# Both feed-forward networks of a decoder layer: gate and up as Strassen's seven products, down as a stage of its own

## The chip, the cores and the metric

One core of one Trainium2 chip runs the whole layer as one program. The metric is the device time of one execution in microseconds (us). TensorE (PE) multiplies matrices into PSUM; VectorE (DVE), ScalarE (ACT) and GpSimd (POOL) do elementwise work; SyncE (SP) issues the DMAs, all on one queue.

## The reference

One step of a decoder layer over 1,024 prompt tokens and 64 sample tokens, 1,088 in all, with a model width of 1,024. The change touches the two half-step feed-forward networks (FFNs), before the token mixing and after it:

```python
def swiglu_half(x, norm_g, w_gate, w_up, w_down):
    u = rmsnorm(x, norm_g)
    return x + 0.5 * ((jax.nn.silu(u @ w_gate) * (u @ w_up)) @ w_down)

h = swiglu_half(x, *ffn1)
# ... input projection, two kinds of windowed attention, cross attention ...
h = swiglu_half(h, *ffn2)
y = rmsnorm(h, final_norm)
```

w_gate and w_up are 1,024 x 2,816, w_down is 2,816 x 1,024. All data are float32.

## The kernel before, in words

Activations lie transposed: model width on the 128 partitions (8 blocks k), tokens along the free axis, in three chunks CH of 384, 384 and 320 tokens. Each float32 operand is split in two parts of TensorE's rounded format, high = round(a) on ScalarE and low = a - high on VectorE, and each product is three matmuls (`mm3`: high x high, high x low, low x high). Weights pass through the class `Weights`: a list `entries` in the order of use, each 128 x 1024; `load` puts the DMA on SP's queue into one of two raw buffers, `split` makes the parts in one of four ring buffers (lines 75 and 76), and `done` frees a ring buffer and goes on with the next.

`ffn` works on one block m of 128 hidden units at a time, 22 in all. The gate of a block: 3 chunks x 8 k x 3 matmuls with the weight block stationary and up to 384 tokens moving, into PSUM. The evacuation (lines 303 to 305) multiplies by the tokens' 1/rms (`rbc`), applies silu and multiplies by `rbc` again; the gain is already in the operand x. Up likewise, then the product and its split into hh and hl. After every two blocks `down` adds their part of the down projection: 8 x 3 groups of six matmuls, each taken out of PSUM by VectorE with `x += 0.5 * p` (line 327). So x stays in SBUF for the whole FFN and collects the sum over 11 parts.

Around it: x tiles come in transposed by TensorE (`before1`); after the last part of FFN 1 each finished block of x is split for the input projection and its squares are summed on GpSimd (`after1`); cross attention's output projection (`o_proj`) ends with the split of x for FFN 2; after FFN 2 x is transposed back, normalized and written (`after2`). A scheduler lays out the instructions of each engine's queue from the program's order and from when operands are ready in its own estimate; each engine then works through its queue in order.

Of the kernel before, what the change touches and what calls it, by code (L numbers as in the profile page):

```python
# [9 lines left out]
F32 = mybir.dt.float32  # L10
# [7 lines left out]
D = 1024  # L18
# [13 lines left out]
CH = [(0, 384), (384, 384), (768, 320)]  # L32
CHB = [(0, 3), (3, 6), (6, 8)]
# [15 lines left out]
class Weights:  # L49
# [30 lines left out]
    def prefetch(self):  # L80
        total = len(self.entries)
# [18 lines left out]
def trunk(ctx, tc, A, O, dbg=None):  # L100
# [30 lines left out]
    def ffn_entries(pre):  # L131
        wg = A[pre + "_w_gate"].rearrange("(k p) f -> p k f", p=128)
        wu = A[pre + "_w_up"].rearrange("(k p) f -> p k f", p=128)
        wd = A[pre + "_w_down"]

        def down(k):
            entries.append((f"{pre}d{k}", [(full, wd[k * 128:(k + 1) * 128, :])], 1024))

        for m in range(MF):
            entries.append((f"{pre}g{m}", [(kview(8), wg[:, :, m * 128:(m + 1) * 128])], 1024))  # L140
            if m % 2 == 0 and m:
                down(m - 2)
# [64 lines left out]
    xscr = [dr.tile([128, KD, NT], F32, name=f"xscr{i}") for i in range(3)]  # L207
# [3 lines left out]
    gains = const.tile([128, 5, KD], F32, name="gains")  # L211
# [5 lines left out]
    rcol = const.tile([128, 9], F32, name="rcol")  # L217
# [4 lines left out]
    ws = Weights(nc, rawp, ringp, entries, RING, RAWB)  # L222

# [22 lines left out]
    def col_sums(psp, ss):  # L246
        p = psp.tile([128, 512], F32, name="pcs", tag="sm")
        for j in range(9):
            PE.matmul(p[:, 2 * j:2 * j + 2], ss[:, j * 128:(j + 1) * 128], ones, start=True, stop=True)
        return p[:, 0:18].rearrange("p (j t) -> p j t", t=2)[:, :, 0]  # L250

    def bcast_rstd(psp):
        for j0, j1 in ((0, 4), (4, 8), (8, 9)):
# [6 lines left out]
    def norm_stats(psp, ss):  # L260
        finish_rstd(rcol, col_sums(psp, ss), 9)
# [18 lines left out]
    def ffn(pre, x, psp, fp, stats, after, order=(0, 1, 2), before=lambda c: None, at=(5, 6)):  # L280
        hh = fp.tile([128, 2, NT], F32R, name="hh", tag="hh")
        hl = fp.tile([128, 2, NT], F32R, name="hl", tag="hl")
        first = [True]

        def chunk(w, c):
            c0, n = CH[c]
            wh, wl = (t[:, :].rearrange("p (k c) -> p k c", k=8) for t in w)
            p = psp.tile([128, 512], F32, name="pmm", tag="mm")
            for k in range(KD):
                mm3(p[:, :n], wh[:, k], wl[:, k], xh[:, k, c0:c0 + n], xl[:, k, c0:c0 + n], k == 0, k == KD - 1)  # L290
            return p

        def proj(name):
            w = ws.get(name)
            out = [chunk(w, c) for c in range(3)]
            ws.done()
            return out

        def gate_evac(pg):
            out = []  # L300
            for (c0, n), p in zip(CH, pg):
                t = fp.tile([128, 384], F32, name="tg", tag="tg", bufs=4)
                V.tensor_tensor(t[:, :n], p[:, :n], rbc[:, c0:c0 + n], op=ALU.mult)  # L303
                S.activation(t[:, :n], t[:, :n], AF.Silu)  # L304
                G.tensor_tensor(t[:, :n], t[:, :n], rbc[:, c0:c0 + n], op=ALU.mult)  # L305
                out.append(t)
            return out

        def up_evac(m, ts, pu):
            for (c0, n), p, t in zip(CH, pu, ts):  # L310
                V.tensor_tensor(t[:, :n], t[:, :n], p[:, :n], op=ALU.mult)  # L311
                a = hh[:, m % 2, c0:c0 + n]
                S.activation(a, t[:, :n], AF.Copy)  # L313
                V.tensor_tensor(hl[:, m % 2, c0:c0 + n], t[:, :n], _b(a), op=ALU.subtract)

        def down(part, last):
            ws_ = [ws.get(f"{pre}d{2 * part + j}") for j in range(2)]

            def one(mo, c):
                c0, n = CH[c]  # L320
                p = psp.tile([128, 512], F32, name="pmm", tag="mm")
                for j in range(2):
                    wh, wl = ws_[j]
                    ms = slice(mo * 128, (mo + 1) * 128)
                    mm3(p[:, :n], wh[:, ms], wl[:, ms], hh[:, j, c0:c0 + n], hl[:, j, c0:c0 + n],
                        j == 0, j == 1)
                V.scalar_tensor_tensor(x[:, mo, c0:c0 + n], p[:, :n], 0.5, x[:, mo, c0:c0 + n],  # L327
                                       op0=ALU.mult, op1=ALU.add)

            if not last:  # L330
                for mo in range(8):
                    for c in range(3):
                        one(mo, c)
            else:
                for c in order:
                    for mo in range(8):
                        one(mo, c)
                        after(mo, c)
            ws.done(2)

        for m in range(MF):
            if m == 0:
                pg, pu = [], []
                for c in range(3):
                    before(c)
                    if c == 0:
                        w = [ws.get(f"{pre}g0"), ws.get(f"{pre}u0")]
                    for i, out in enumerate((pg, pu)):
                        if 2 * c + i == at[0]:
                            stats()  # L350
                        if 2 * c + i == at[1]:
                            bcast_rstd(psp)
                        out.append(chunk(w[i], c))
                ws.done(2)
                if at[1] == 6:
                    bcast_rstd(psp)
                ts = gate_evac(pg)
            else:
                pg = proj(f"{pre}g{m}")
                ts = gate_evac(pg)  # L360
                if m % 2 == 0:
                    down(m // 2 - 1, False)
                pu = proj(f"{pre}u{m}")
            up_evac(m, ts, pu)
        down(MF // 2 - 1, True)


    ss = const.tile([128, 1152], F32, name="ss")
    with ExitStack() as ph:
        xp = ph.enter_context(pool(name="xp", bufs=1))  # L370
        fp = ph.enter_context(pool(name="fp", bufs=1))
        psp = ph.enter_context(pool(name="ps1", bufs=6, space=PSUM))
        pss = ph.enter_context(pool(name="ps1s", bufs=2, space=PSUM))

        class Both:
            def tile(self, shape, dt, name, tag):
                return (pss if tag == "sm" else psp).tile(shape, dt, name=name, tag=tag)

        both = Both()
        x = xp.tile([128, KD, NT], F32, name="x")  # L380
        ssum = const.tile([128, 9], F32, name="ssum")
        V.memset(ssum, 1.0)
        V.memset(ss[:, 1088:1152], 1.0)
        xin = ph.enter_context(pool(name="xin", bufs=3))

        def load_x(t):
            rows = 128 if t < 8 else 64
            xi = xin.tile([128, D], F32, name="xi", tag="xi")
            SP.dma_start(out=xi[:rows, :], in_=A["x_prompt"][t * 128:(t + 1) * 128, :] if t < 8 else A["x_sample"])
# [1223 lines left out]
```

## Time and profile before

| | us |
|---|---|
| three runs | 2671.40, 2671.79, 2675.32 (median 2671.79) |
| the profiled execution | 2664.77 |
| its span | 2663.0 |
| PE busy in the span | 2590.8 (97%) |
| DVE busy | 1291.2 (48%) |
| ACT busy | 835.0 (31%) |
| POOL busy | 472.6 (18%) |
| PE's granted clock, mean | 0.992 of full |

The span runs from the first to the last instruction; the rest of the execution's time lies around it. PE's busy time counts matmuls from issue to modelled end, and these overlap: what a matmul costs is read from the distance of two starts.

### The profile page before, as it was taken

How to read it: one execution, taken by the hardware profiler on the slowest of the kernel's cores; microseconds unless marked ns; L12 is line 12 of the kernel's file. 1: busy time of each engine (PE TensorE's matmuls, PEld its weight loads, DVE VectorE, ACT ScalarE, POOL GpSimd, SP SyncE). 2: the span in 40 equal slices, each digit the busy share in tenths (PEclk: the TensorE clock that was granted, in tenths of full speed). 3: DMA queues.
4: the chain of work that ended last, by engine and by line, in shares of the span. 5: the costliest groups of instructions: out<-in, count | busy, mean ns of one | idle time of the engine just before them, and what ended most of it. 6: DMA issues, size and time to landing. Idle time of an engine off the chain costs nothing.

```text
span 2663.0 us, 39413 instructions
## 1 busy us (share of the span) xinstructions
PE 2590.8 (97%) x15802; PEld 2496.0 (94%) x15802; DVE 1291.2 (48%) x2694; ACT 835.0 (31%) x1585; POOL 472.6 (18%) x557
## 2 busy tenths in 40 slices
PE   8999999999999899999899899998999999999998
PEld 7999999999998678899798899998999999999998
DVE  5444443443444424468687544487343444444444
ACT  6111111111124124457566334365211111111113
POOL 1001111111105732100234232002110001110011
PEclk9999999999999999999899999999999999999999
DMA  4111111111124846633221462525311111111111
GB/s 132 48 48 40 48 34 47 48 48 48 40 68 153 279 142 192 190 93 95 72 62 59 137 209 87 159 80 185 124 48 40 48 43 46 48 40 48 47 33 68
DMA packets 239303, 231.42 MB, mean 87 GB/s; under 512 B 11688, under 2 KB 208400, under 8 KB 239120
## 3 DMA queue, kind: packets, MB, share of 16 engines
q1 hardware_dynamic: 239120, 228.91, 27.5%
q8 instruction: 124, 2.03, 0.3%
q14 instruction: 59, 0.48, 0.1%
HBM read 186.86 MB, written 42.01 MB: 86 GB/s over the span
## 4 chain that ended last, share of the span: by engine, by line
PE 86%; DVE 6%; DMA 4%; ACT 2%; issue 1%; POOL 1%; SPq 0%; DVEq 0%; ACTq 0%; POOLq 0%
PE pmm L229 19%; PE pmm L231 19%; PE pmm L230 19%; PE pb L229 2%; PE pb L230 2%; PE pb L231 2%; PE pf L229 2%; PE pf L231 2%; PE pf L230 2%; DMA qb<-zqs 1%; DVE wlo L76 1%; DVE xl L268 1%; PE pS L897 1%; PE pS L898 1%; PE pO L229 1%
## 5 line engine op out<-in xcount | busy, mean ns | idle before, releaser
L229 PE MATMUL pmm<-xh,whi 128*128 128x384 f32 (+1 forms) x2112 | 689.2, 327 | 3.2 <-DVE xo L1277 2.0
L230 PE MATMUL pmm<-xl,whi 128*128 128x384 f32 (+1 forms) x2112 | 689.7, 327 | 0.0
L231 PE MATMUL pmm<-xh,wlo 128*128 128x384 f32 (+1 forms) x2112 | 689.4, 326 | 0.0
L75 ACT ACTIVATE whi<-wraw 128x1024 fp32r<-128x1024 f32 (+2 forms) x236 | 237.5, 1020 | 737.4 <-PE pmm L230 620.2
L229 PEld LDWEIGHTS pmm<-xh,whi 128*128 128x128 f32 x2112 | 397.0, 188 | 4.1 <-ACT xh L267 4.0
L305 POOL TENSOR_TENSOR tg<-tg,rbc 128x384 f32<-128x384 f32 x132 | 156.7, 1187 | 1369.1 <-ACT tg L304 1347.9
L230 PEld LDWEIGHTS pmm<-xl,whi 128*128 128x128 f32 x2112 | 397.1, 188 | 0.1
L231 PEld LDWEIGHTS pmm<-xh,wlo 128*128 128x128 f32 x2112 | 397.1, 188 | 0.0
L327 DVE SCALAR_TENSOR_TENSOR x<-pmm,x 128x384 f32<-128x384 f32 (+1 forms) x528 | 278.0, 534 | 202.9 <-PE pmm L231 202.7
L229 PE MATMUL pmm<-hh,whi 128*128 128x384 f32 (+1 forms) x1056 | 346.4, 329 | 0.0
L231 PE MATMUL pmm<-hh,wlo 128*128 128x384 f32 (+1 forms) x1056 | 346.3, 328 | 0.0
L230 PE MATMUL pmm<-hl,whi 128*128 128x384 f32 (+1 forms) x1056 | 346.0, 328 | 0.0
L76 DVE TENSOR_TENSOR wlo<-wraw,whi 128x1024 fp32r<-128x1024 f32 (+2 forms) x236 | 279.9, 1198 | 111.3 <-ACT whi L75 110.7
L303 DVE TENSOR_TENSOR tg<-pmm,rbc 128x384 f32<-128x384 f32 x132 | 70.5, 535 | 333.9 <-PE pmm L231 333.9
L230 PEld LDWEIGHTS pmm<-hl,whi 128*128 128x128 f32 x1056 | 198.4, 188 | 0.1
L231 PEld LDWEIGHTS pmm<-hh,wlo 128*128 128x128 f32 x1056 | 198.4, 188 | 0.0
L229 PEld LDWEIGHTS pmm<-hh,whi 128*128 128x128 f32 x1056 | 198.2, 188 | 0.2
L311 DVE TENSOR_TENSOR tg<-tg,pmm 128x384 f32<-128x384 f32 x132 | 70.2, 532 | 258.9 <-PE pmm L231 254.2
L313 ACT ACTIVATE hh<-tg 128x384 fp32r<-128x384 f32 x132 | 66.2, 502 | 305.6 <-DVE tg L311 305.6
L304 ACT ACTIVATE tg<-tg 128x384 f32<-128x384 f32 x132 | 66.1, 502 | 297.3 <-DVE tg L303 297.3
L277 POOL TENSOR_TENSOR ss<-ss,sq 128x384 f32<-128x384 f32 (+1 forms) x63 | 72.0, 1142 | 271.3 <-ACT sq L276 264.0
L229 PE MATMUL pf<-xh,whi 128*128 128x384 f32 (+1 forms) x336 | 113.6, 338 | 3.7 <-DVE tg L814 3.1
(432 smaller groups left out, 4301.3 us busy)
## 6 DMA issues: line engine op xcount, KB each, us to landing
wraw<-ffn_w_gate SPq DMA_DIRECT2D x44, 512.0 KB, 3.9
wraw<-ffn_w_up SPq DMA_DIRECT2D x44, 512.0 KB, 3.9
wraw<-ffn_w_down SPq DMA_DIRECT2D x44, 512.0 KB, 4.2
wraw<-w_in SPq DMA_DIRECT2D x32, 512.0 KB, 4.2
wraw<-cache_dil_v SPq DMA_DIRECT2D x24, 512.0 KB, 4.5
k<-cache_dil_k SPq DMA_DIRECT2D x16, 512.0 KB, 5.1
zscr<-z SPq DMA_DIRECT2D x32, 256.0 KB, 4.6
qb<-zqs SPq DMA_DIRECT2D x16, 512.0 KB, 5.3
```

The lines of the kernel that those rows point to most:

```text
L75: self.nc.scalar.activation(hi[:, :w], t[:, :w], AF.Copy)
L76: self.nc.vector.tensor_tensor(lo[:, :w], t[:, :w], _b(hi[:, :w]), op=ALU.subtract)
L229: PE.matmul(out, lh, rh, start=first, stop=False)
L230: PE.matmul(out, lh, rl, start=False, stop=False)
L231: return PE.matmul(out, ll, rh, start=False, stop=last)
L277: G.tensor_tensor(ss[:, d0:d0 + n], ss[:, d0:d0 + n], q[:, :n], op=ALU.add)
L303: V.tensor_tensor(t[:, :n], p[:, :n], rbc[:, c0:c0 + n], op=ALU.mult)
L304: S.activation(t[:, :n], t[:, :n], AF.Silu)
L305: G.tensor_tensor(t[:, :n], t[:, :n], rbc[:, c0:c0 + n], op=ALU.mult)
L311: V.tensor_tensor(t[:, :n], t[:, :n], p[:, :n], op=ALU.mult)
L313: S.activation(a, t[:, :n], AF.Copy)
L327: V.scalar_tensor_tensor(x[:, mo, c0:c0 + n], p[:, :n], 0.5, x[:, mo, c0:c0 + n], op0=ALU.mult, op1=ALU.add)
```

## The change

Tokens are taken in two halves of 544, each as two quarters of 272 (H). With weights in four quadrants (two halves of the model width kh, two hidden blocks fh) and the normalized x in four quadrants B11, B21, B12, B22 (width half, token quarter), a unit (half s, pair j of hidden blocks) forms seven products of a sum of weight quadrants with a sum of x quadrants instead of eight products of quadrants; each product is 2 (gate, up) x 4 k x 3 matmuls of 272 columns, in four pairs of PSUM banks X, Y, Z, W. Products 0 and 2 add up in X, 1 and 3 in Y, 4 and 6 in Z, and 5 is in W; evacuations combine them. The operands are now normalized (gain and 1/rms) before their split. GpSimd forms the weight sums S1 to S4; x sums T1 to T4 are made by VectorE for the first half and by GpSimd for the second, whose x quarters are made in hooks between units. All weights of gate and up are loaded and split once per half. The hidden activations go to DRAM (hscr).

Down follows as a stage: chunk by chunk, h comes back from DRAM and is split, and each of 8 output blocks contracts over all 22 hidden blocks in one PSUM group; its weights come as 72 entries (24 per chunk). x comes back from DRAM for the residual. The input projection's operands are split after the stage; the split at the end of `o_proj` goes; the final norm works per chunk, with sums of squares and gain in the transposed layout. The core of the diff:

```diff
+H = 272
+PROD = [("X", "A11", "B11"), ("Y", "S2", "T2"), ("X", "A12", "B21"), ("Y", "S3", "T3"), ("Z", "S1", "T1"),
+        ("W", "A22", "T4"), ("Z", "S4", "B22")]
+FIRST = (0, 2, 1, 3, 4, 5, 6)
+class Quads:
...
+    def load(self):
...
+        for q, kh, fh in (("A11", 0, 0), ("A12", 1, 0), ("A21", 0, 1), ("A22", 1, 1)):
+            t = self.rawp.tile([128, 1024], F32, name="r" + q, tag="r" + q, bufs=2)
...
+    def sums(self, u):
+        r = self.raw[u]
+        r["S1"] = self.sump.tile([128, 1024], F32, name="wraw", tag="wraw")
+        self.nc.gpsimd.tensor_tensor(r["S1"], r["A21"], r["A22"], op=ALU.add)
+        self.nc.gpsimd.tensor_tensor(r["A21"], r["A11"], r["A21"], op=ALU.subtract)
+        r["S3"] = r["A21"]
+    def split(self):
...
+        self.nc.scalar.activation(hi, r[q], AF.Copy)
+        self.nc.vector.tensor_tensor(lo, r[q], _b(hi[:, :]), op=ALU.subtract)
+        self.parts[n] = (hi, lo)
+        if q == "A11":
+            self.nc.gpsimd.tensor_tensor(r["A11"], r["S1"], r["A11"], op=ALU.subtract)
+            r["S2"] = r["A11"]
+        elif q == "A12":
+            self.nc.gpsimd.tensor_tensor(r["A12"], r["A12"], r["S2"], op=ALU.subtract)
+            r["S4"] = r["A12"]
+        elif q == "S1":
+            if self.n_load < MF:
+                self.load()
+            if u + 1 < MF:
+                self.sums(u + 1)
...
+        for c in range(3):
+            for mo in range(8):
+                for g, (k0, nk) in enumerate(((0, 8), (8, 8), (16, 6))):
+                    entries.append((f"{pre}d{c}.{mo}.{g}", [
...
+    class Operands:
...
+        def sums1(self, E):
...
+            E.tensor_tensor(self.flat("T1"), self.flat("B12"), self.flat("B11"), op=ALU.subtract)
+            E.tensor_tensor(self.flat("T2"), self.flat("B22"), self.flat("T1"), op=ALU.subtract)
+        def sums2(self, E):
+            E.tensor_tensor(self.flat("B12"), self.flat("B22"), self.flat("B12"), op=ALU.subtract)
+            self.slots["T3"] = self.slots["B12"]
+            E.tensor_tensor(self.flat("B11"), self.flat("T2"), self.flat("B21"), op=ALU.subtract)
+            self.slots["T4"] = self.slots["B11"]
+        def split(self, s, nm):
+            r = row(s, nm)
+            S.activation(xh[:, r], self.flat(nm), AF.Copy)
+            V.tensor_tensor(xl[:, r], self.flat(nm), _b(xh[:, r]), op=ALU.subtract)
+    def products(pre, quads, ops, psA, tp, hook):
+        def unit(s, j):
...
+            def evac(i, g, p):
+                _, c12, c21, c22 = c[g]
+                if i == 0:
+                    S.activation(c22, p, AF.Copy)
+                elif i == 1:
+                    V.tensor_tensor(c12, c22, p, op=ALU.add)
+                elif i == 2:
+                    if g == 0:
+                        S.activation(c[0][0], p, AF.Silu)
+                    else:
+                        V.tensor_tensor(c[0][0], c[0][0], p, op=ALU.mult)
+                elif i == 3:
+                    V.tensor_tensor(c21, c22, p, op=ALU.add)
+                elif i == 4:
+                    V.tensor_tensor(c22, c21, p, op=ALU.add)
+                elif i == 5:
+                    V.tensor_tensor(c21, c21, p, op=ALU.subtract)
+                else:
+                    V.tensor_tensor(c12, c12, p, op=ALU.add)
+                    if g == 0:
+                        S.activation(t[:, H:4 * H], t[:, H:4 * H], AF.Silu)
+                    else:
+                        G.tensor_tensor(t[:, H:4 * H], t[:, H:4 * H], v, op=ALU.mult)
+                        SP.dma_start(out=hscr[j][s][:, :, :].rearrange("p q c -> p (q c)"), in_=t)
+            for i in (range(7) if s or j else FIRST):
...
+                for g in range(2):
+                    new = (b, g) not in ps
+                    if new:
+                        ps[b, g] = psA.tile([128, 512], F32, name="p" + b, tag=b, bufs=2)
+                    p = ps[b, g][:, :H]
+                    for k in range(4):
+                        PE.matmul(p, wh[:, g, k], bh[:, k], start=new and k == 0, stop=False, skip_group_check=True)
+                        PE.matmul(p, wh[:, g, k], bl[:, k], start=False, stop=False, skip_group_check=True)
+                        PE.matmul(p, wl[:, g, k], bh[:, k], start=False, stop=(k == 3), skip_group_check=True)
+                for g in range(2):
+                    evac(i, g, ps[b, g][:, :H])
+                quads.done()
+                if s == 0 and j == MF // 2 - 1 and i < 6:
+                    ops.split(1, PROD[i + 1][2])
+            hook(s, j)
+    def down(pre, resid, after, stack):
...
+        def load_h(c, j):
...
+                        SP.dma_start(out=st[:, :, o:o + e - b], in_=hscr[j][s][:, :, b - 544 * s:e - 544 * s])
...
+            split2(h, l, st[:, :, :n])
...
+            for mo in range(8):
+                p = psp.tile([128, 512], F32, name="pd", tag="pd")
+                for g in range(3):
+                    w = ws.get(f"{pre}d{c}.{mo}.{g}")
+                    for q in range(8 if g < 2 else 6):
+                        k = 8 * g + q
...
+                        mm3(p[:, :n], w[0][:, cs], w[1][:, cs], hh, hl, k == 0, k == MF - 1)
+                    ws.done()
+                V.scalar_tensor_tensor(xs[c][:, mo, :n], p[:, :n], 0.5, xs[c][:, mo, :n], op0=ALU.mult, op1=ALU.add)
+                after(mo, c, xs)
...
+        def hook1(s, j):
...
+            if j in (2, 3):
+                trans(j + 4, "W")
...
+            if j == 6:
+                ops.split(1, "B11")
+                ops.sums1(G)
+            if j == 7:
+                ops.sums2(G)
...
-                    for k in range(KD):
-                        split_x(xo, 3, k, 0, n, c0)
...
+        ops2 = Operands(ph2, 1)
+        norm_stats(smallps, ss, 0, 6)
+        bcast_rstd(smallps, ((0, 4), (4, 6)))
+        x_load2(ops2, 0)
+        x_norm2(ops2, 0)
+        for nm in ("B11", "B21"):
+            ops2.split(0, nm)
         run(o_proj(2))
+        norm_stats(smallps, ss, 6, 9)
+        bcast_rstd(smallps, ((6, 9),))
         pa.close()
...
+        quads = Quads(nc, rawl, rawp, ringp, A["ffn2_w_gate"], A["ffn2_w_up"])
+        quads.start()
+        quads.prefetch()
...
+            if j == 2:
+                x_norm2(ops2, 1)
```

## Rows read from the trace of the kernel before

**Rows 1.** The profile's page: engine shares, and shares of the chain that ended last.

```profile
PE 2590.8 (97%) x15802; PEld 2496.0 (94%) x15802; DVE 1291.2 (48%) x2694; ACT 835.0 (31%) x1585; POOL 472.6 (18%) x557
...
PE 86%; DVE 6%; DMA 4%; ACT 2%; issue 1%; POOL 1%; SPq 0%; DVEq 0%; ACTq 0%; POOLq 0%
```

**Rows 2.** Busy by stretch: each engine's us (xcount), clock, DMA share, GB/s.

```profile
60.00:700.00 640.00, 640.00 (x3877) 640.00 (x3876) 263.30 (x432) 107.14 (x162) 64.39 (x54) 1.00 0.15 45
```

**Rows 3.** Timeline, PE: start us, us, engine, line, operation, shapes.

```profile
299.69 0.31 PE L230 MATMUL pmm<-xl,whi 128*128 128x320 f32 x1
...
300.87 0.33 PE L229 MATMUL pmm<-hh,whi 128*128 128x384 f32 x1
...
302.97 0.31 PE L229 MATMUL pmm<-hh,whi 128*128 128x320 f32 x1
```

**Rows 4.** Timeline, PE, fifteen matmuls of 256 columns: first and last.

```profile
1725.53 0.28 PE L229 MATMUL pS<-mkh,xh 128*128 128x256 f32 x1
...
1727.18 0.28 PE L231 MATMUL pX<-KHc,QPc 128*64 128x256 f32 x1
```

**Rows 5.** Groups by form, ACT: line, names, shapes, count, busy, mean, idle.

```profile
L75 ACT ACTIVATE whi<-wraw 128x1024 fp32r<-128x1024 f32 x212 | 221.3, 1057 | 726.0 <-PE pmm L230 620.2 <-DMA wraw<-w_in 24.7 <-PE pS L664 16.3
```

**Rows 6.** Timeline, DVE, 296 to 345 us.

```profile
302.02 1.23 DVE L76 TENSOR_TENSOR wlo<-wraw,whi 128x1024 fp32r<-128x1024 f32 x1 [0.46 <-ACT whi L75]
303.16 1.41 DVE L327 SCALAR_TENSOR_TENSOR x<-pmm,x 128x384 f32<-128x384 f32 x3
...
325.51 2.36 DVE L76 TENSOR_TENSOR wlo<-wraw,whi 128x1024 fp32r<-128x1024 f32 x2
```

**Rows 7.** Groups by form, DVE.

```profile
L327 DVE SCALAR_TENSOR_TENSOR x<-pmm,x 128x384 f32<-128x384 f32 x352 | 193.9, 556 | 153.4 <-PE pmm L231 153.2
L327 DVE SCALAR_TENSOR_TENSOR x<-pmm,x 128x320 f32<-128x320 f32 x176 | 85.8, 489 | 49.5 <-PE pmm L231 49.5
```

**Rows 8.** Groups by form, POOL.

```profile
L543 POOL TENSOR_TENSOR qb<-qb,k 128x1024 f32<-128x1024 f32 x16 | 39.9, 2496 | 17.9 <-DMA qb<-zqs 14.2 <-DVE ST L545 1.4 <-issue 1.2
...
L980 POOL TENSOR_TENSOR Sm<-Sm 128x640 f32<-128x640 f32 x16 | 25.0, 1565 | 61.1 <-ACT Sm L978 57.8 <-DVE PT L226 2.4 <-DVE Sm L983 0.9
```

**Rows 9.** Timeline, POOL, 866 to 873 us.

```profile
867.88 2.34 POOL L543 TENSOR_TENSOR qb<-qb,k 128x1024 f32<-128x1024 f32 x1 [0.58 <-DMA qb<-zqs]
870.18 1.44 POOL L480 TENSOR_TENSOR r<-z,cs 128x128 f32<-128x128 f32 x1
...
872.25 0.46 POOL L484 TENSOR_TENSOR z<-r,r 128x128 f32<-128x128 f32 x1
```

**Rows 10.** Timeline, DVE, the same stretch.

```profile
868.53 2.78 DVE L76 TENSOR_TENSOR wlo<-wraw,whi 128x1024 fp32r<-128x1024 f32 x1
```

**Rows 11.** Line 305 on POOL (min/median/max ns), and one of its operations.

```profile
L305 POOL TENSOR_TENSOR tg<-tg,rbc x132: 876/1017/1745, 49.7 to 2608.8; 128x384 f32<-128x384 f32 x88, 128x320 f32<-128x320 f32 x44
...
302.48 1.50 POOL L305 TENSOR_TENSOR tg<-tg,rbc 128x320 f32<-128x320 f32 x1 [2.65 <-ACT tg L304]
```

**Rows 12.** Timeline, PE, transposes of a later x tile beside matmuls.

```profile
19.16 0.60 PE L405 MATMUL pmm<-ident,xi 128*128 128x128 f32 x4
19.51 0.43 PE L230 MATMUL pmm<-xl,whi 128*128 128x384 f32 x1
```

**Rows 13.** Timeline, PE, the last matmul of the first FFN.

```profile
813.37 0.34 PE L231 MATMUL pmm<-hh,wlo 128*128 128x384 f32 x1
```

**Rows 14.** Busy by stretch, the first 20 us.

```profile
0.00:10.00 10.00, 3.83 (x16) 3.00 (x16) 1.60 (x6) 4.96 (x8) 0.20 (x4) 1.00 0.79 251
10.00:20.00 10.00, 8.52 (x40) 7.66 (x39) 7.73 (x13) 8.85 (x18) 0.00 (x0) 1.00 0.86 278
```

**Rows 15.** Timeline, PE, the second FFN's first matmul.

```profile
1858.86 0.41 PE L229 MATMUL pmm<-xh,whi 128*128 128x384 f32 x1 [1.99 <-DVE xo L1277]
```

**Rows 16.** DMA issues: count, KB each, median us to landing.

```profile
wraw<-ffn_w_gate SPq DMA_DIRECT2D x44, 512.0 KB, 3.9
...
xi<-x_prompt SPq DMA_DIRECT2D x8, 512.0 KB, 5.3
```

More of the change, by code (lines that the diff above doesn't have):

```diff
@@ L277, in squares @@
             G.tensor_tensor(ss[:, d0:d0 + n], ss[:, d0:d0 + n], q[:, :n], op=ALU.add)
[L280 to L288, printed above, removed]
-            for k in range(KD):
[L290 to L365, printed above, removed]
@@ L1182, in trunk, with x_load2, x_norm2 @@
         return
+    ph2 = ctx.enter_context(ExitStack())
+    def x_load2(ops, s):
+        for nm, hf, c0 in QUARTERS[s]:
+            SP.dma_start(out=ops.slot(nm, new=True), in_=xscr[2][:, 4 * hf:4 * hf + 4, c0:c0 + H])
+    def x_norm2(ops, s):
+        for nm, hf, c0 in QUARTERS[s]:
+            for q in range(4):
+                t = ops.slot(nm)[:, q]
+                V.scalar_tensor_tensor(t, t, gains[:, 3, 4 * hf + q:4 * hf + q + 1], rbc[:, c0:c0 + H],
+                                       op0=ALU.mult, op1=ALU.mult)
     MS = 128.0 ** -0.5
@@ L1501, in after2 @@
[L1501 to L1509 removed]
+        pq = ph.enter_context(ExitStack())
+        rawl = pq.enter_context(pool("rawl2"))
+        tp = pq.enter_context(pool("tp2"))
+        ops2.sump = pq.enter_context(pool("q2s"))
@@ new lines, in trunk, with hook2 @@
+        psA = pq.enter_context(pool("psA2", 2, PSUM))
+        quads = Quads(nc, rawl, rawp, ringp, A["ffn2_w_gate"], A["ffn2_w_up"])
+        quads.start()
+        quads.prefetch()
+        ops2.sums1(V)
+        ops2.split(0, "T2")
+        ops2.sums2(V)
+        for nm in ("T3", "T1", "T4", "B22"):
+            ops2.split(0, nm)
+        def hook2(s, j):
+            if s:
+                return
+            if j == 1:
+                x_load2(ops2, 1)
+            if j == 2:
+                x_norm2(ops2, 1)
+            if j == 3:
+                ops2.split(1, "B11")
+                ops2.sums1(G)
+            if j == 4:
+                ops2.sums2(G)
@@ L1510, in after2 @@
+        def after2(mo, c, xs):
+            x, n = xs[c], sum(m for _, m in DC[c])
+            squares2(sqp, x, mo, c)
+            V.tensor_scalar(x[:, mo, :n], x[:, mo, :n], gains[:, 5, mo:mo + 1], None, op0=ALU.mult)
+            if c and mo == 0:
+                norm(c - 1, xs[c - 1])
             if c == 2 and mo == 7:
-                last(c)
-        ffn("ffn2", x, both, fp, lambda: norm_stats(pss, ss), after2, at=AT)
+                norm(c, x)
+        ws.prefetch()
+        down("ffn2", xscr[2], after2, ph)
```

450 lines of the change are left out of this document (290 added, 160 removed).

## The prediction

> **What bounds the kernel now.** I read the page's engine shares and chain first, then the matmul timeline, then the busy time by stretch, then the other engines' operations by form. [rows 1]: TensorE is busy 97% of the span and is 86% of the chain that ended last; VectorE is at 48%, GpSimd at 18%. From 60 to 700 us [rows 2] TensorE has no gap: 3,877 matmuls in 640 us, 165.1 us per thousand. So an FFN costs what its matmuls cost, and the spacing of matmuls by width is the number to take. [rows 3]: eight of 320 columns take 1.18 us (147 ns each), the twelve of 384 behind them 2.10 us (175 ns). [rows 4]: fourteen steps of 256 columns with other weights each time take 1.65 us (118 ns). These lie on a line (0.45 ns per column), so 272 columns cost 125 ns; no floor from the weight loads shows at 256, hence none is to be expected at 272.
>
> **Gate and up.** Before, per FFN: 22 blocks x 2 x 3 chunks x 8 k x 3 = 3,168 matmuls x 165.1 ns = 523 us. After: 22 units (2 halves x 11) x 7 products x 2 x 4 k x 3 = 3,696 x 125 ns = 462 us, 21.0 us per unit, 3.0 us per product. That is -61 us per FFN, -122 us for both. (The Trainium skill, "TensorE: Matmul & The Clock Gate", section "Back-to-back issue gap", puts the isolated gap at columns/2.4 + 2.5 ns. The trace has 11 to 15 ns above columns/2.4, so here the measurement decides; by the page's figure the gain would be an estimated 117 us.) Down keeps its 1,584 matmuls of 384 and 320 columns per FFN: 0.
>
> **What now has to fit into 21.0 us per unit.** This is where I expect the gain to go. ScalarE: seven splits x 1.06 [rows 5] and four evacuations, together some 9.5 us; fits. VectorE: seven low parts x 1.18 us (back to back, [rows 6]: 2.36 for two) = 8.3, and eleven PSUM evacuations. Three of 384 columns back to back take 1.41 us [rows 6], 0.47 each; 384 against 320 [rows 7] gives 1.05 ns per column, so 272 take 0.35 back to back and 0.42 alone: five pairs of 0.75 and one of 0.42, 4.2 us. VectorE's own work is 12.4 us. GpSimd: S1, S2, S3, S4 of 1024 columns at 2.37 and the product with up of 816 columns, 1.95 (2.2 ns per column between [rows 8]'s forms): 11.4 us.
>
> These two are not independent. [rows 9] and [rows 10]: the low part at 868.53 takes 2.78 us instead of 1.2 because GpSimd is at its addition until 870.2; GpSimd's next, at 870.18, then takes 1.44 us where its like takes 0.46, until VectorE's ends. One of them runs, the other stands still for the whole instruction. [rows 11]: an operation of 320 columns, 0.88 at its fastest, takes 1.50 when it starts under the low part of 302.02, but isn't slowed by the three evacuations out of PSUM at 303.16. So low parts and sums exclude each other, evacuations don't. The shared time is 8.3 + 11.4 = 19.7 of 21.0 us, and VectorE works in order: an evacuation queued behind a low part that stands still waits too.
>
> How long VectorE takes then: its own 12.4 us, and for each GpSimd operation the time it stands, less the evacuation that falls beside it. S2 can't start before the low part of A11 ends, and S2's split needs it and then ScalarE: 2.37 + 1.06 + 0.1 for the two signals - 0.75 = 2.8. S4: 2.37 - 0.75 = 1.6. The product: 1.95 with nothing beside it. S1 and S3 of the next unit: behind S4 and the product 1.6 + 1.95 = 3.5; in the time that S2's split takes anyway 1.2 + 1.6 = 2.8. That is 22.3 or 21.6 us a unit. The order of the queues is by readiness, not by the program: transposes of later x tiles stand among the matmuls [rows 12], and S1 and S3 are ready early. I take 21.6: +0.6 x 44 = **+26**. Below, 0 (TensorE keeps the pace); above, 22.5 with signals, +66. (The Trainium skill, "SBUF — State Buffer", section "Who interferes with whom", speaks against such a division of work: the one that issues second is blocked until the first is done, and a VectorE operation with one SBUF input doesn't contend. Rows 9 to 11 show the same; by the rule alone the sum would be what it is here, between 0 and the upper bound.) Where TensorE then waits: product 3 accumulates in the bank that product 1's evacuation must first read, and that evacuation stands behind S1's low part.
>
> **The second half's operands**, made in the first half's units, come on top of a VectorE that has no slack. FFN 1: 48 small operations that read PSUM, about 8 us, of which half can fall beside a GpSimd sum, with two rstd chains 5 in all; seven operand splits of 1088 columns x 1.25 = 8.8; four GpSimd sums of 2.54 that hold VectorE about 1.8 each = 7: 21 us. FFN 2: 16 normalizations at about 0.4 = 6.4 in place of the transposes' share: 22 us. Together **+43**; if there is slack, 6 each, 12, for the unit that carries six splits.
>
> **Start of FFN 1.** Before, its last matmuls are at 813.4 [rows 13], 4,752 of them cost 785 us: 29 us lost to the start and the transposes. After: x tiles 0 to 2 and the gains land at about 8 us (1.5 MB at [rows 14]'s 250 to 280 GB/s and 2 us), but 4 MB of weights stand in the same queue ahead of tile 4, which lands near 25; square, rstd, broadcast 4 us, normalization 2.5, T1 and T2 2.4, split 2.4: T2 near 38 to 40. Only A11.B11 and A12.B21 can run before, 6 us. So TensorE is dense from about 40 with 6 us done: 34 lost, 4.4 more for the forty transposes in the hooks: 38, **+9** (0 to +18).
>
> **Start of FFN 2.** Before, TensorE waits 2.0 us ahead of FFN 2's first matmul [rows 15]; its weights were already split. After, its raw tiles take over the SBUF of pools that close at that point. If they come free only then: A11 and A12 land after 4 to 6 us (512 KB take 3.9, [rows 16]), split 2.3, two products, then the wait for A21 and A22, S1, S3, S2 one after the other (7.1) and a split: 10 to 20 us. If free under the last output projection, near 0. I take **+12**, as the tiles of that projection are in use to its end.
>
> **The rest.** Gate to down, +3 per FFN: weights and h of chunk 0 (written a half earlier) can be loaded under the last unit, h splits follow the rows that products release; bounds 0 and 10. The end of FFN 1: x can be split for the projection only when chunk 2's h, in the same tiles, is read: +3 (0 to 8). Tail: the last squares are added up by GpSimd, 1.0 us for 384 columns [rows 11], where ScalarE summed them with the squaring, +1. Together **+10**. Down itself has less VectorE work (24 evacuations per FFN in the place of 264) and is TensorE's if its weights come: see the third rival.
>
> Sum: -122 + 26 + 43 + 9 + 12 + 10 = -22. The profiled execution took 2664.8 us (span 2663.0), so 2643; the runs' median is 7 higher, 2671.8, and there I forecast **2650**.
>
> **Rivals.** (1) TensorE sets the pace: VectorE catches up because the splits run four products ahead. For it: 19.7 of 21.0 fits. Against: in-order waiting. 2650 - 26 - 31 = 2593. (2) Slower: the exclusion between VectorE and GpSimd costs the late order, with S1, S3 and the product one behind the other, 22.5 us per unit: +40, 2690. The place is TensorE's wait for the Y bank at product 3 of each unit; it decides from about 22 us a unit on, where the sum crosses zero. (3) Down's weights: read three times, 72 entries per FFN through two raw buffers. A buffer's turn is 3.9 us to land and 2.3 to split, 3.1 per entry, against 3.64 of matmuls. At 5.3 us to land, as x tiles of the same size take beside other traffic [rows 16], it is 3.8: +0.16 x 144 = +23, 2673, no change. That the change doesn't do what it says I exclude: the matmul count is fixed by the loops.
>
> **How the numbers follow.** Forecast 0.40 (its own range 2620 to 2670), rival 1 0.26, rival 2 0.24, rival 3 0.10. Two tenths of a per cent, 5 us, is about what this kernel's runs can tell from no change. Faster: 0.26 + 0.37 = 0.63; within: 0.03 of the forecast and 0.07 of rival 3 = 0.10; slower 0.27. The range goes from a little under rival 1 to a little over rival 2: 2588 to 2700.
>
> **What would show it.** Matmuls of 272 columns 125 ns apart, and products 3.0 us long except one per unit that waits for VectorE; low parts of 1.2 us and others of 2 to 3.6; units 21.5 us or so in the second half, longer in the first. Wrong if units are 21.0 throughout (rival 1), over 22 (rival 2), if matmuls are not at 125, or if down's matmuls wait for low parts of weights (rival 3).

## The result, and the profile after

The changed kernel takes 2741.4 us (median of four runs, 2739.2 to 2747.0) against 2671.6 of the kernel before in the same session: ratio 1.0265, 95% interval 1.0243 to 1.0288. It is slower, by 70 us; the forecast was 2650, with a range that ended at 2700.

First the page of the changed kernel, engine shares (busy us, share of the span, instructions):

```profile
span 2737.9 us, 44133 instructions
PE 2523.8 (92%) x16885; PEld 2412.5 (88%) x16885; DVE 1704.9 (62%) x2841; ACT 1172.6 (43%) x1895; POOL 970.3 (35%) x681
```

Beside [rows 1]: TensorE is busy 67 us less, in a span 75 us longer. So the products did save matmul time, and TensorE now stands still for some 214 us (before, 72). No other engine is near full. The question is who waits for whom.

The matmuls are as forecast. Four in a row of the timeline (start, duration, engine, line):

```profile
304.36 0.29 PE L453 MATMUL pZ<-xh,whi 128*128 128x272 f32 x1
304.48 0.29 PE L454 MATMUL pZ<-xl,whi 128*128 128x272 f32 x1
304.61 0.29 PE L455 MATMUL pZ<-xh,wlo 128*128 128x272 f32 x1
304.74 0.29 PE L453 MATMUL pZ<-xh,whi 128*128 128x272 f32 x1
```

They are 0.12 to 0.13 us apart; a unit that waits for nothing takes 21.2 us (168 x 126 ns). Next the stages of the changed kernel, cut where TensorE goes from one to the next (columns: stretch; its us; busy us and count of TensorE, weight loads, VectorE, ScalarE, GpSimd; granted clock; DMA share; GB/s):

```profile
0.00:570.60 570.60, 502.03 (x3787) 491.64 (x3788) 428.48 (x548) 248.33 (x320) 303.84 (x117) 0.96 0.44 132
570.60:834.20 263.60, 261.76 (x1586) 260.41 (x1585) 125.08 (x141) 109.50 (x152) 35.92 (x28) 1.00 0.67 199
834.20:1888.40 1054.20, 1003.26 (x6137) 912.50 (x6136) 585.62 (x1524) 487.85 (x1013) 275.13 (x390) 0.98 0.42 134
1888.40:1930.00 41.60, 2.34 (x13) 2.02 (x11) 34.66 (x36) 12.79 (x15) 27.81 (x11) 0.53 0.69 183
1930.00:2194.60 264.60, 241.94 (x1850) 237.90 (x1849) 196.98 (x213) 102.52 (x126) 154.20 (x56) 0.98 0.37 111
2194.60:2451.90 257.30, 239.21 (x1850) 236.57 (x1849) 191.93 (x212) 105.24 (x130) 137.03 (x52) 0.99 0.42 126
2451.90:2723.80 271.90, 267.64 (x1645) 266.66 (x1644) 137.20 (x161) 103.56 (x136) 35.33 (x28) 1.00 0.60 174
2723.80:2737.90 14.10, 5.56 (x32) 4.78 (x31) 4.96 (x11) 2.85 (x5) 0.99 (x1) 0.75 0.42 112
```

These are: gate and up of FFN 1, its down, everything between the FFNs, the hole ahead of FFN 2, gate and up of FFN 2 in two halves, its down, the end. The forecast of each follows from the terms of the prediction (for instance FFN 1's gate and up: 813.4 - 61 + 13 + 21 + 9 - 261.5 of down's 1,584 matmuls at 165.1 ns = 533.9):

| stage, us | forecast | after | e1 (below) |
|---|---|---|---|
| gate and up, FFN 1 | 533.9 | 570.6 | 531.2 |
| down, FFN 1 | 264.5 | 263.6 | 265.7 |
| between the FFNs | 1046.2 | 1054.2 | 1057.5 |
| hole ahead of FFN 2 | 14.3 | 41.6 | 24.7 |
| gate and up, FFN 2 | 497.0 | 521.9 | 494.5 |
| down, FFN 2, with the last transposes | 269.7 | 271.9 | 269.1 |
| end | 15.4 | 14.1 | 14.0 |
| span | 2641.0 | 2737.9 | 2656.7 |

Of the 97 us too many, 89 stand in gate and up and the hole ahead of FFN 2; down is right to 2 us. TensorE's waits in the changed kernel (line waited for and its releaser: us in total, times, longest):

```profile
PE pY L453 <- DVE tg L421: 58.5, 36, 2.3
PE pT L334 <- POOL ss L362: 20.7, 1, 20.7
PE pT L341 <- DVE rcol L329: 18.6, 1, 18.6
PE pY L455 <- DVE wlo L155: 6.9, 9, 1.6
```

The first is the wait for the Y bank at product 3, 36 times in 44 units, 1.6 us each; the next two are the hole. In the steady part of a second half a unit takes 23.1 us where TensorE would need 21.2.

Why product 3 waits is read one queue further back. The same kernel's waits of the other two engines in the loop:

```profile
ACT whi L154 <- POOL rA L158: 305.2, 42, 12.3
POOL wraw L143 <- DMA rA<-ffn_w_up: 218.6, 30, 15.5
```

One unit of FFN 2's second half of the changed kernel, GpSimd's queue first, then ScalarE, VectorE and TensorE (in brackets the idle time before, and what ended it):

```profile
2400.85 2.38 POOL L143 TENSOR_TENSOR wraw<-rA,rA 128x1024 f32<-128x1024 f32 x1 [6.92 <-DMA rA<-ffn_w_up]
2403.31 2.40 POOL L144 TENSOR_TENSOR rA<-rA,rA 128x1024 f32<-128x1024 f32 x1
2405.66 2.40 POOL L158 TENSOR_TENSOR rA<-wraw,rA 128x1024 f32<-128x1024 f32 x1
2410.95 2.76 POOL L438 TENSOR_TENSOR tg<-tg,tv 128x816 f32<-128x816 f32 x1 [2.89 <-ACT tg L436]
2413.67 3.37 POOL L161 TENSOR_TENSOR rA<-rA,rA 128x1024 f32<-128x1024 f32 x1
2424.13 2.40 POOL L158 TENSOR_TENSOR rA<-wraw,rA 128x1024 f32<-128x1024 f32 x1 [7.08 <-DVE wlo L155]
2408.09 2.01 ACT L154 ACTIVATE whi<-rA 128x1024 fp32r<-128x1024 f32 x2 [8.42 <-POOL rA L158]
2399.70 1.23 DVE L155 TENSOR_TENSOR wlo<-rA,whi 128x1024 fp32r<-128x1024 f32 x1 [0.53 <-ACT whi L154]
2409.19 1.23 DVE L155 TENSOR_TENSOR wlo<-rA,whi 128x1024 fp32r<-128x1024 f32 x1 [2.44 <-ACT whi L154]
2410.68 4.12 DVE L155 TENSOR_TENSOR wlo<-rA,whi 128x1024 fp32r<-128x1024 f32 x2
2414.72 3.41 DVE L155 TENSOR_TENSOR wlo<-wraw,whi 128x1024 fp32r<-128x1024 f32 x1
2418.05 0.42 DVE L421 TENSOR_TENSOR tg<-tg,pY 128x272 f32<-128x272 f32 x1
2418.53 0.39 PE L453 MATMUL pY<-xh,whi 128*128 128x272 f32 x1 [1.67 <-DVE tg L421]
```

L143 and L144 are S1 and S3, L158 is S2, L438 the product with up, L161 S4. The S1 at 2400.85 belongs to the unit after the next, and its weights have only just landed. S2 of the next unit stands behind it and S3. S2 overwrites A11, so it can't start before A11's low part (2399.70) ends at 2400.93; by then S1 is running. So of GpSimd's 6.9 idle us S2 loses nothing, but it stands behind the run time of S1 and S3 and starts 4.7 us late, at 2405.66. Had S1's weights landed those 4.7 us earlier, both sums would have run in the idle time. The last S2 of the FFN has no S1 ahead of it, and starts 0.08 us after A11's low part, at 2424.13.

With S2 its split is late, the low parts behind that in VectorE's queue (three of them lengthened, since GpSimd now catches up beside them), and the evacuation of 2418.05 that frees Y. The weights are late for their part because the raw buffer of A22 comes free only when its low part is taken, which stands behind that evacuation. It closes on itself: the reading is that one turn takes 23.1 us whatever TensorE could do. (The Trainium skill, "TensorE: Matmul & The Clock Gate", row "Engine queue depth" of the table at its head, calls the queues of ScalarE, VectorE and GpSimd strictly first in, first out. The trace agrees: S3 starts at 2403.31, ahead of an S2 that has been ready since 2400.93.)

### The profile page after: what moved, and what is told of

Its sections match the earlier page's. It is cut to its first block, busy times and chain, and to the rows that moved or that the text cites. A ratio compares the mean times of both kernels' runs of the same rounds, so it can differ in the third digit from the quotient of the medians.

```text
span 2737.9 us, 44133 instructions
## 1 busy us (share of the span) xinstructions
PE 2523.8 (92%) x16885; PEld 2412.5 (88%) x16885; DVE 1704.9 (62%) x2841; ACT 1172.6 (43%) x1895; POOL 970.3 (35%) x681
## 5 line engine op out<-in xcount | busy, mean ns | idle before, releaser
L154 ACT ACTIVATE whi<-rA 128x1024 fp32r<-128x1024 f32 x264 | 273.9, 1055 | 535.4 <-POOL rA L158 305.2
L155 DVE TENSOR_TENSOR wlo<-rA,whi 128x1024 fp32r<-128x1024 f32 x264 | 411.6, 1568 | 116.2 <-ACT whi L154 115.3
L453 PE MATMUL pY<-xh,whi 128*128 128x272 f32 x704 | 213.4, 304 | 65.1 <-DVE tg L421 58.5
L316 PE MATMUL pd<-xh,wlo 128*128 128x384 f32 x704 | 235.6, 335 | 0.2 <-DVE wlo L78 0.2
L314 PE MATMUL pd<-xh,whi 128*128 128x384 f32 x704 | 235.7, 335 | 0.0
L315 PE MATMUL pd<-xl,whi 128*128 128x384 f32 x704 | 235.5, 334 | 0.0
L143 POOL TENSOR_TENSOR wraw<-rA,rA 128x1024 f32<-128x1024 f32 x44 | 120.8, 2746 | 307.2 <-DMA rA<-ffn_w_up 218.6
L455 PE MATMUL pY<-xh,wlo 128*128 128x272 f32 x704 | 210.0, 299 | 6.9 <-DVE wlo L155 6.9
L453 PE MATMUL pX<-xh,whi 128*128 128x272 f32 x704 | 207.5, 295 | 4.7 <-ACT xh L401 1.6
L454 PE MATMUL pY<-xl,whi 128*128 128x272 f32 x704 | 207.9, 296 | 0.0
L455 PE MATMUL pX<-xh,wlo 128*128 128x272 f32 x704 | 205.9, 292 | 0.0
L438 POOL TENSOR_TENSOR tg<-tg,tv 128x816 f32<-128x816 f32 x44 | 118.6, 2696 | 123.8 <-ACT tg L436 122.2
L161 POOL TENSOR_TENSOR rA<-rA,rA 128x1024 f32<-128x1024 f32 x44 | 139.7, 3174 | 30.1 <-issue 15.2
## 6 DMA issues: line engine op xcount, KB each, us to landing
wraw<-ffn_w_down SPq DMA_DIRECT2D x96, 512.0 KB
wraw<-w_in SPq DMA_DIRECT2D x32, 512.0 KB
wraw<-cache_dil_v SPq DMA_DIRECT2D x24, 512.0 KB
```

Of the source, the lines that this page charges most:

```text
L143: self.nc.gpsimd.tensor_tensor(r["S1"], r["A21"], r["A22"], op=ALU.add)
L154: self.nc.scalar.activation(hi, r[q], AF.Copy)
L155: self.nc.vector.tensor_tensor(lo, r[q], _b(hi[:, :]), op=ALU.subtract)
L161: self.nc.gpsimd.tensor_tensor(r["A12"], r["A12"], r["S2"], op=ALU.subtract)
L314: PE.matmul(out, lh, rh, start=first, stop=False)
L315: PE.matmul(out, lh, rl, start=False, stop=False)
```

## Experiments

My theory: S1's and S3's place in GpSimd's queue costs the 23.1. Rival A: the exclusion of VectorE and GpSimd costs it (rival 2 of the prediction, only dearer). Rival B: the load of the weights. "Eleven units" are the last eleven of an FFN, from product W to product W; the first of them still carries hooks in most kernels, and TensorE alone needs 233. Where several runs were timed the ratio to before is given, since the medians of before go from 2665 to 2672 between sessions.

**e1: S1 in one buffer of its own**, so that it can't be made before the S1 of the unit ahead has been split.

```diff
-        r["S1"] = self.sump.tile([128, 1024], F32, name="wraw", tag="wraw")
+        r["S1"] = self.rawp.tile([128, 1024], F32, name="rS1", tag="rS1", bufs=1)
```

> S1 gets one buffer of its own, so that S1 and S3 of the unit after next cannot stand ahead of S2 in GpSimd's queue. Theory A (order): the 23.1 us of a unit is a loop from A22's low part over the weight DMA, S1, S3, S2, its split and S1's low part to product 3's wait; with S2 first the units fall to 21.2 to 22.3 us, the time to 2665 to 2705. Theory B (exclusion alone: low parts and GpSimd sums hold each other up, in whatever order): units stay at 22.9 or more, 2725 to 2745.

2653.5 us, ratio 0.9947 (0.9928 to 0.9967): with this one line the change is half a per cent faster than before. Eleven units take 239.4 and 237.9 us (after: 257.3 and 258.8), 21.3 each but the first, as theory A said; the time is better than its 2665 to 2705. A unit of e1 in FFN 2's second half, VectorE and then GpSimd:

```profile
2312.54 3.01 DVE L155 TENSOR_TENSOR wlo<-rA,whi 128x1024 fp32r<-128x1024 f32 x1
2315.47 2.97 DVE L155 TENSOR_TENSOR wlo<-rS,whi 128x1024 fp32r<-128x1024 f32 x1
2319.05 2.95 DVE L155 TENSOR_TENSOR wlo<-rA,whi 128x1024 fp32r<-128x1024 f32 x1
2322.27 3.07 DVE L155 TENSOR_TENSOR wlo<-rA,whi 128x1024 fp32r<-128x1024 f32 x1
2325.96 1.21 DVE L155 TENSOR_TENSOR wlo<-rA,whi 128x1024 fp32r<-128x1024 f32 x1
2330.85 2.36 DVE L155 TENSOR_TENSOR wlo<-rA,whi 128x1024 fp32r<-128x1024 f32 x2 [2.20 <-ACT whi L154]
2333.82 3.02 DVE L155 TENSOR_TENSOR wlo<-rA,whi 128x1024 fp32r<-128x1024 f32 x1
2312.06 2.40 POOL L161 TENSOR_TENSOR rA<-rA,rA 128x1024 f32<-128x1024 f32 x1 [3.62 <-DVE wlo L155]
2314.41 2.94 POOL L438 TENSOR_TENSOR tg<-tg,tv 128x816 f32<-128x816 f32 x1
2318.51 2.41 POOL L143 TENSOR_TENSOR rS<-rA,rA 128x1024 f32<-128x1024 f32 x1 [1.16 <-DMA rA<-ffn_w_gate]
2321.00 3.27 POOL L144 TENSOR_TENSOR rA<-rA,rA 128x1024 f32<-128x1024 f32 x1
2327.32 2.40 POOL L158 TENSOR_TENSOR rA<-rS,rA 128x1024 f32<-128x1024 f32 x1 [3.06 <-DVE wlo L155]
```

GpSimd's order is now S4, product, S1, S3, S2, and S1, S3 and S2 are all for the same next unit, whose weights have landed: the "late order" that the prediction priced at 22.3 and feared. S1 and S3 are done before A11's low part (2325.96) ends at 2327.18, and S2 starts 0.14 us behind that, where it was 4.7 us late. Four low parts of seven do stand under a GpSimd operation (3.0 us instead of 1.2), and VectorE waits 2.2 us for S2's split; from 2312.54 to 2333.82 that makes 21.28. So the exclusion is there as forecast, but it all but fits into TensorE's 21.2.

**e2: a third raw buffer for A22**, so that the weights of a later unit can be asked for before the chain's end.

```diff
-            t = self.rawp.tile([128, 1024], F32, name="r" + q, tag="r" + q, bufs=2)
+            t = self.rawp.tile([128, 1024], F32, name="r" + q, tag="r" + q, bufs=3 if q == "A22" else 2)
```

> A third raw buffer for A22, GpSimd's order nearly as it is. Theory A: S1's wait for its weights (6.9 us a unit) shrinks by the 2 to 3 us that A22's DMA is issued earlier, units about 22, time about 2700. Theory B: no wait for weights matters, 2735 to 2745.

2682.0 us (one run), units mostly of 21.2 to 22.6, eleven in 248.2 and 246.4. That is better than the 2700 that theory A expected. The queue is as in the changed kernel, but its head waits less (4.5 to 5.6 us), and S2 starts 2.2 us behind A11's low part: opening the loop at its other end gives back about half in these units. S2 late by 4.7, 2.2 and 0.1 us goes with steady units of 23.1, about 21.8 and 21.3. The wait for the weights and the order are two halves of one cause; rival B holds only in so far as the order makes a transfer matter.

**e5: low parts of the weights on ScalarE** (the remainder left out: the low part is a copy of the weight), so that nothing of VectorE's in the loop needs the shared turn for weights.

```diff
-        self.nc.vector.tensor_tensor(lo, r[q], _b(hi[:, :]), op=ALU.subtract)
+        self.nc.scalar.activation(lo, r[q], AF.Copy)
```

> The low parts of gate and up weights are made by ScalarE (as copies, the remainder is left out), so that VectorE's weight work no longer excludes GpSimd. Theory A: the loop loses the 3.9 us in which two low parts stand behind GpSimd, units 21.2, time about 2655. Theory B: the same, as the exclusion is gone; if units stay over 22 the exclusion is no part of the cause and the weight DMA with GpSimd's order is all of it.

2677.6 us (one run); eleven units 248.7 and 249.2, most at 21.2 and every second to fourth at 23 to 27. With the exclusion gone, S1 and S3 ahead of S2 alone still cost 16 us per half. TensorE's wait has moved: it is now for ScalarE's evacuation of X (23.3 us, 19 times), as ScalarE does the low parts too and its splits wait for S2 (220.6 us in all). Theory A's units of 21.2 throughout and 2655 are missed.

**e6: e1 and e5 together.**

> Both at once: S1 in its own buffer and the weights' low parts on ScalarE (copies, the remainder left out). Theory A (order of GpSimd's queue behind a weight DMA costs 1.8 us a unit, the exclusion by itself next to nothing once the order is right): the second half, 239 us with the order alone, comes to 233 (eleven units of 21.2), the time to 2635 to 2645. Theory B (the exclusion is a cost of its own): 10 us or more per half beyond that, below 2630.

2626.7 us (one run), eleven units 233.1 and 233.0: TensorE's pace, to 0.1 us, as theory A had it; the time is in theory B's range, since FFN 1's start and first half gain 5.6 us more on e1, and the stretch from the last cross matmul to FFN 2's gate and up another 10.9. With e1 and e5 this is a full two-by-two for the eleven units (FFN 1 / FFN 2):

| | low parts on VectorE | on ScalarE |
|---|---|---|
| S1, S3 a unit early (after) | 257.3 / 258.8 | 248.7 / 249.2 |
| S1, S3 late (e1) | 239.4 / 237.9 | 233.1 / 233.0 |

The order costs 18 to 21 us with the low parts on VectorE and 16 without; the low parts' place on VectorE costs 9 to 10 with the early order and 5 to 6 with the late. That second price is of the exclusion and of VectorE's own 8 us of low parts together: the experiment doesn't part them. And of the 5 to 6 all but about 1 us falls in the first of the eleven units, the one with hooks (26.5 and 25.0 in e1, 21.2 in e6). The theory stands; rival A has a share, a smaller one.

**e4, e8: the last statistics of FFN 2 moved** behind its first unit, to see whether they make the hole (e4 on the changed kernel, e8 on e1).

```diff
-        norm_stats(smallps, ss, 6, 9)
-        bcast_rstd(smallps, ((6, 9),))
...
+            if j == 0:
+                norm_stats(StatsW(), ss, 6, 9)
+                bcast_rstd(StatsW(), ((6, 9),))
```

> The last third's norm statistics move from ahead of FFN 2's first products into the hook of unit 0. Both theories: TensorE's two waits of 20.7 and 18.6 us there go, and the first products wait for their own operands only, some 12 to 15 us: 2710 to 2720. If the time stays, the first products were not ready earlier.

> S1 in its own buffer and the last statistics in unit 0's hook. If FFN 2's start waits for VectorE's operands, TensorE's waits of 16.5 and 6.0 us only move: 2645 to 2653. If the statistics hold it, 15 to 20 us go: 2635.

e4: 2736.4, ratio 1.0261 (1.0245 to 1.0278), where after had 1.0265. e8: 0.9971 (0.9956 to 0.9987), not better than e1. The first product does come 31 us earlier (1899.3 for 1930.0 in the changed kernel), but e4's gate and up end at 2453, where they ended at 2452: the next units take 33 and 26 us instead. The expectation of e4 is missed, and e8's 2658.5 lies above both that were named. The wait is put down to the statistics; that what TensorE lacked were operands fits, and e7 bears it out in part.

**e7: low parts of x on ScalarE, on e1** (remainder left out as in e5).

```diff
-            V.tensor_tensor(xl[:, r], self.flat(nm), _b(xh[:, r]), op=ALU.subtract)
+            S.activation(xl[:, r], self.flat(nm), AF.Copy)
```

> S1 in its own buffer, and the low parts of the x operands on ScalarE (copies, remainder left out): 14 operations of 1.25 us per FFN less on VectorE. If the starts of both FFNs and the half switch wait for VectorE's queue, 8 to 15 us per FFN go: 2625 to 2640. If they wait for DMA and the rstd chain: 2648 or more.

2630.9 us (one run), eleven units 234.6 and 234.9. FFN 1's first product W starts at 57.0, in e1 at 58.7: the low parts of x don't set that start. Elsewhere they count, and the first branch of the expectation holds: FFN 1's gate and up end 7.5 us earlier than in e1 (the unit of 26.5 us ahead of the switch falls to 21.2), and the stretch from the end of the last cross matmul to the end of FFN 2's gate and up is 506.0 us, in e1 518.9.

**e9: the second half's x sums on VectorE, on e1** (`sums1(V)`, `sums2(V)` for `G` in both hooks).

> S1 in its own buffer and the second half's x sums on VectorE (1.3 us each) in the place of GpSimd (2.5): by theory A the shared time of the two units before the switch falls by 5 us and their waits (4 to 6 us in each FFN) shrink: 2643 to 2650. If VectorE's own time is what counts there: 2653 to 2660.

2648.0, ratio 0.9932 (0.9899 to 0.9966), which e1's interval doesn't exclude; eleven units 237.9 twice. The time is as theory A expected, but not by its way: in FFN 2 the two units before the switch take 24.9 and 25.0, as in e1.

**e10: in e9 the product with up on VectorE too; e11: in e9 the third block's x loaded ahead of the weights; e12: both.**

```diff
-                        G.tensor_tensor(t[:, H:4 * H], t[:, H:4 * H], v, op=ALU.mult)
+                        V.tensor_tensor(t[:, H:4 * H], t[:, H:4 * H], v, op=ALU.mult)
```

```diff
-            t = rawp.tile([128, D], F32, name="wraw", tag="wraw") if i == 3 else \
+            t = rawp.tile([128, D], F32, name="wraw", tag="wraw") if i in (3, 4) else \
...
-        quads.load()
...
+        load_x(4)
+        quads.load()
```

> e9 with the stage's product (silu times up, 128x816) moved from GpSimd to VectorE. If what still lies above TensorE's 21.2 us in a unit of e9 (237.9 against 233 us for eleven units) is GpSimd's turn with VectorE, the product's 2.0 to 2.8 us leave that turn, VectorE gets about 1 us more, and eleven units take 233 to 235: time 2638 to 2645. Rival: VectorE is the fuller engine of the loop, its 1 us more comes late at the next eviction, units 21.6 or more, time 2650 to 2660.

> e9 with FFN1's third block's x (tiles 3 and 4) loaded ahead of both weight quads, into two of the weights' buffers. In e9 the third block's squares come only at about 30 us and its scaled copies at 39 us, and the first sums of x at 45 us. If the start hangs on that transfer, the sums come some 10 us earlier and product W of the first unit, at 58 us in e9, begins at about 48 to 50: time 2636 to 2642. If VectorE's and ScalarE's own work in the first 55 us sets the start, or the weights that now come later take its place, W begins at 54 us or later and the time is 2645 to 2652. Loops unchanged (237.9 for eleven units) by either.

> e10 and e11 together: 2628 to 2640 if both hold, with eleven units in 233 to 235 us; 2645 or more if neither does. By the sum of parts the time is e9's plus the two differences that e10 and e11 show.

e10: 2637.7, ratio 0.9895 (0.9875 to 0.9915). Ten of the eleven units are at 21.2; the one with hooks takes 26.3 and 25.4, so that the eleven still read 238.2 and 237.3, not 233 to 235. The product takes 1.2 us on average on VectorE, where on GpSimd it took 2.7 on average in the changed kernel. e11: 2652.4, 0.995 (0.993 to 0.997): W starts at 58.2, as in e9 (58.3), so that transfer alone isn't the bound; the weights now land later, and whether they take its place isn't parted here. e12: 2643.5, 0.9921 (0.9897 to 0.9945), as the two together let expect.

**e13: on e10, the running sum of squares of the last output projection on VectorE**, since in e10 the last of these sums stands behind an S1 on GpSimd.

```diff
-                squares(sqp, ss, xo, m, 0, n, c0)
+                squares(sqp, ss, xo, m, 0, n, c0, V if c == 2 else G)
```

> e10 with the running sum of squares of the last output projection (seven additions of 320 columns, about 0.46 us each on VectorE) on VectorE in place of GpSimd. In e10 TensorE's hole between the last cross matmul (1839.47) and FFN2's first product (1864.84) is 25.4 us; 19.8 of it ends with the last of these sums, which stands on GpSimd behind an S1 that takes 7.8 us (2.4 alone) because VectorE's operations run back to back. If GpSimd's waiting for a turn is the cause, the last sum comes at about 1850 to 1853 and the hole shrinks to 15 to 20 us: time 2628 to 2634. Rival: the first products wait for VectorE's and ScalarE's operands anyway; the hole moves into the first unit, the sums only make VectorE's queue longer, time 2636 to 2642. Loops as in e10 by either (237 to 238 us for eleven units).

2636.7, 0.9890 (0.9866 to 0.9914), as e10. The hole grew to 36.4 us (1837.97 to 1874.36; e10: 25.4) and the first units gave it back: from the last cross matmul to the end of gate and up 512.0 us, in e10 510.7. The rival holds. Where the last square went, on ScalarE of e13:

```profile
1858.14 2.00 ACT L154 ACTIVATE whi<-rA 128x1024 fp32r<-128x1024 f32 x2 [11.71 <-POOL rA L158]
1860.05 0.45 ACT L361 ACTIVATE sq<-xo 128x320 f32<-128x320 f32 x1
```

The last square, 0.45 us of work, stands behind a split that waits 11.7 us for S2: the same trap as in the loop, in another queue.

## Why the prediction was wrong, point by point

- **The failed step** is "S1 and S3 are ready early. I take 21.6". It took their early place in the queue as a gain, because they would then run in the time in which S2's split is under way. It says itself that S2 can't start before A11's low part ends, and didn't ask whether their weights land before that. They land just then: S1 and S3 run ahead of S2, which starts 4.7 us late in a steady unit, and the unit grows from 21.2 to 23.1. Measured 23.1 early and 21.3 late, where 21.6 and 22.3 were expected: even the order of the two was the wrong way round. Undoing it takes the span from 2737.9 to 2656.7, 81 of the 97 us.
- **Matmuls of 272 columns at 125 ns, -122 us**: right (125 to 126; a unit 21.2 for 21.0).
- **Exclusion of VectorE and GpSimd** [rows 9 to 11]: the mechanism is right, a little over-priced. The late order's sum was 12.4 of VectorE's own + 2.8 + 1.6 + 1.95 + 3.5 = 22.3. e1's unit has 11.9 + 2.2 of waiting + four low parts at 1.78 more than their 1.14, 7.1 = 21.3. (The Trainium skill, "SBUF — State Buffer", section "Who interferes with whom", says what these rows say: two SBUF inputs contend, one doesn't.)
- **Second half's operands, 43**: over-priced once the order is right. In e1 the units with hooks exceed 21.3 by some 17 in FFN 1 (forecast 21 + 4.4 for transposes) and by 7.3 in FFN 2 (forecast 22).
- **Start of FFN 1, +9**: under-priced by some 12. In e1 TensorE is dense from product W at 58.7 on, with four products of 3.03 done, so 46.5 us are lost; forecast 34. What sets it is open: neither x's transfer alone (e11) nor x's low parts on VectorE alone (e7).
- **Start of FFN 2, +12**: the largest other miss. Hole and slow first units take 41.6 us and more in the changed kernel; in e1 the hole is 24.7 and gate and up then lose another 18.6 (494.5 - 22 x 21.3 - 7.3), 43 together, for 14.3. I counted transfers and one chain of S1, S3, S2, and not the normalization, splits and sums that VectorE and GpSimd do there in turns: VectorE is busy 34.7 of the hole's 41.6 us. e4, e8 and e13 fit this work as the bound, and not the statistics: each moved the waiting, and none shortened the stretch by more than 2 us. e7, which takes x's low parts off VectorE, shortens it by 12.9, of which 3 lie in the eleven units; so they are a part of the bound. Which part of the rest comes last is open.
- **Between the FFNs, +3**: measured 8 more than forecast, in e1 11. In the kernel before, the first matmuls of the input projection stood among the last of FFN 1 (from 802.9 on); in the changed one they start behind it. I didn't separate the rest.
- **Down, 0, with +3**: right. Rival 3 isn't there: in FFN 1's down TensorE waits 1.8 us in all.
- **The rivals**: rival 2 named the right place, the wait for Y at product 3, and a decisive point of 22 us a unit; its cause, the late order, is refuted by e1. Rival 1 is what e6 shows as soon as both causes are gone. The 2650 of the forecast is nearly e1's 2653.5, but e1 has the late order, its profiled span is 15.7 us over the forecast's, and its stages miss with both signs, so that isn't a confirmation.

The best version run is e10 (e13 is no different), 1.05% faster than before (ratio 0.9875 to 0.9915); e6's 2626.7, with the weights' remainders left out, lies 11 us lower, but lacks e9's and e10's moves, so the gap isn't the price of the exclusion.

## What to carry to other kernels

An operation that is free to run early isn't free in an in-order queue: ask what it waits for, and what stands behind it, before you count its early place as a gain. One buffer less can be the cure, since a buffer that comes free too soon lets an instruction be placed ahead of more urgent work in a queue where it waits for a transfer. And a wait that TensorE puts down to one small chain (statistics) is worth testing by moving the chain: where the hole moves along, the work behind it is the bound.

## What the runs showed of the hardware that was not expected

**GpSimd can be kept from its turn for several operations.** At FFN 2's start in the changed kernel:

```profile
1896.26 9.17 POOL L143 TENSOR_TENSOR wraw<-rA,rA 128x1024 f32<-128x1024 f32 x1 [5.34 <-DVE xo L1540]
1897.28 2.35 DVE L155 TENSOR_TENSOR wlo<-rA,whi 128x1024 fp32r<-128x1024 f32 x2
1899.55 2.48 DVE L402 TENSOR_TENSOR xl<-B,xh 128x1088 fp32r<-128x1088 f32 x2
1901.95 1.28 DVE L390 TENSOR_TENSOR T<-B,B 128x1088 f32<-128x1088 f32 x1
1905.39 0.85 POOL L362 TENSOR_TENSOR ss<-ss,sq 128x320 f32<-128x320 f32 x1
1909.38 3.42 DVE L391 TENSOR_TENSOR T<-B,T 128x1088 f32<-128x1088 f32 x1 [6.16 <-POOL ss L362]
1912.72 3.44 DVE L394 TENSOR_TENSOR B<-B,B 128x1088 f32<-128x1088 f32 x1
```

An S1 of 2.4 us takes 9.17 because VectorE's operations with two SBUF inputs follow each other without a gap until 1903.2; GpSimd gets on when VectorE stops. Later both alternate, and then each of VectorE's takes 3.4 instead of 1.3. The prediction had them take turns from the start.

**A lower clock can follow a short wait of TensorE.** Windows of the changed kernel around product 3 of one unit (columns as in the stages):

```profile
296.00:300.70 4.70, 2.96 (x23) 2.74 (x23) 4.70 (x3) 3.83 (x5) 2.25 (x1) 0.99 0.85 266
300.70:304.20 3.50, 3.50 (x18) 3.50 (x17) 3.50 (x6) 0.00 (x0) 0.00 (x0) 0.52 0.39 112
304.20:310.00 5.80, 5.80 (x48) 5.80 (x47) 5.80 (x7) 3.19 (x3) 3.01 (x1) 1.00 0.55 160
```

Behind a wait of 1.74 us that ended at 299.73, TensorE runs for 3.5 us at 0.52 of full clock, the 1.2 GHz level; its matmuls are 227 ns apart instead of 126, and the wait costs 1.6 us more than itself. The trace has four such drops in each FFN's loop, each behind a wait of 1.4 to 2.3 us; most waits of the same length have none. Over the span the granted clock is 0.971, in the kernel before 0.992.
